# Gate rows replicated through the matrix engine, and bias bands written one group at a time, in a hybrid mLSTM and attention layer

## The chip, the cores and the metric

The kernel runs on one core of a Trainium2 chip. The metric is device time in microseconds of one execution of the whole layer. TensorE (PE, with its weight loads PEld), VectorE (DVE), ScalarE (ACT) and GpSimd (POOL) each work through an instruction queue of their own, in order; SyncE (SP) issues the weight loads from device memory, and POOL issues the other DMAs.

## The reference, cut to what matters

One layer over 256 tokens of width 1024, in float32. A combined projection feeds two mixers; the change touches the operands of both.

```
mLSTM (4 heads x 256):  d[q,s] = F[q] - F[s] + i[s]      (F: running sum of log f)
                        m[q]   = running maximum, the stabiliser
                        w[q,s] = exp(d[q,s] - m[q]) for s <= q
                        h      = (q k^T * w) v / max(|sum|, exp(-m))
attention (8 heads x 128): p = softmax(q k^T / sqrt(128) + bias[head, q - k]), causal
                           bias from a 32-bucket table of distances
x <- LayerNorm(a x + mixer(x));  x <- LayerNorm(a x + conv-gated MLP(x))
```

In the kernel G = i - F and M is the running maximum of G, so the weight of a pair is exp(G[s] - M[q]). It needs -M along the free axis, the same in all 128 partitions, a row of 256 numbers for each of the 4 heads. The bias of two attention heads is a tile `toe` of 128 x 2 x 256: partition p holds the bias row shifted by p places.

## The kernel before, in words

The weights come as 66 blocks of 1 MB, in the order of a list ("steps"): 4 blocks `o`, then four groups of eight (`qm`, `qb`, `km`, `kb`, `vm`, `vb`, `ga`, `gb`), then the branch and output projections and the MLP. A group is one mLSTM head and two attention heads. In step s PE multiplies block s with the activations; each matrix is split into a high and a low part (`wh`, `wl`), by ACT and DVE, two steps ahead, and a product is three matmuls (`mm3`, L124 to L126). SP loads block s+5 in step s into one of three `raw` buffers.

All orders are written by hand. For each step there is a list of element-wise work (`side_elem`, or a `mixed` list that interleaves it with the split), which is issued to ACT, DVE and POOL before the step's matmuls, and a list of small matmuls (`side_pe`) that PE does behind the step's own. Below, "b+4" is the fifth step of a group, its `vm`.

- `rel_bias_expand`, in step 4 (the first group's `qm`): DVE writes the table `ev`; POOL sends it to device memory (`table`, L499) and issues four copies there (`band`, L501), one for each group, in which each of the group's two rows is repeated 128 times. `load_band` (L354) reads a band with a row length one shorter than it was written with, which gives the shift by partition, into `toe`. For group 0 it stands in `open_att`, which runs when step 8 begins, for the others in b+1.
- `gates_schedule`: `e1d` (step b+2 of group 0) makes -M on DVE (L548, 4 x 256). POOL sends it to device memory (`rowscr`, L552) and reads it back into all partitions (`nM`, 128 x 4 x 256, L554).
- `group_schedule`, side work of PE: in b+4 `pe_s` (scores `pss`) and `pe_l(0)` (logits `psl` of the first attention head); in b+5 `pe_l(1)` and `pe_n` (the mLSTM's `psn`, from `sph`, `spl` and `vmh`, `vml`); in b+6 `pe_t` (`pst`).
- In b+5 the element-wise order is: `vtmp` (DVE); `el_w` (ACT's two Exp of `nM` give `wt`, L599 and L600, then POOL's causal mask, L601); `el_l(0)` (DVE adds `toe` to the logits, L702); the split of `vtmp`; `el_e(0)` (ACT); `el_s` (DVE multiplies `wt` with the scores, L608; ACT rounds to `sph`, L612); `el_l2(0)`; `el_s2` (`spl`); then `floor` and the split of a weight block.

Small results of PE go through five PSUM buffers in turn (`ps_side`), the steps' own through three others. `att`, the pool of `toe`, `wt`, `lg` and the like, opens in step 8, where the space of the pool `pre` becomes free.

Of the kernel before, what the change touches and what calls it, by code (L numbers as in the profile page):

```python
# [10 lines left out]
F32 = mybir.dt.float32  # L11
# [3 lines left out]
ALU = mybir.AluOpType  # L15
# [3 lines left out]
P = 128  # L19
S = 256  # L20
D = 1024
KT = D // P
NG = 4
# [8 lines left out]
LTOE = 384  # L32
# [37 lines left out]
class Kernel:  # L70
# [100 lines left out]
    def run(self):  # L171
        tc, nc, ctx = self.tc, self.nc, self.ctx
# [3 lines left out]
        dram = ctx.enter_context(tc.tile_pool(name="dram", bufs=1, space=DRAM))  # L176
# [6 lines left out]
        mp = mix_cm.__enter__()  # L183
# [53 lines left out]
        g = nc.gpsimd  # L237
# [18 lines left out]
        g.memset(self.vml[:, :, 256:258].bitcast(F32), 0.0)  # L256
        self.cbuf = mp.tile([P, 2, S + 3], F32, name="cbuf")
        g.memset(self.cbuf[:, :, 0:3], 0.0)
        self.cv = {n: mp.tile([P, 2, S], F32, name="cv" + n) for n in ("qm", "km")}
        self.ones4 = xp.tile([4, 2 * S], F32, name="ones4")  # L260
        g.memset(self.ones4[:, 0:S], 1.0)
# [19 lines left out]

        self.bands = [dram.tile([2, P * LTOE], F32, name=f"band{i}") for i in range(NG)]
        self.table = dram.tile([8, LTOE], F32, name="table")
        self.rowscr = dram.tile([4, S], F32, name="rowscr")

        att_cm = tc.tile_pool(name="att", bufs=1)
        post_cm = tc.tile_pool(name="post", bufs=1)
# [57 lines left out]
    def open_att(self, ap):  # L345
        self.ap = ap
        self.pt = [(ap.tile([P, 2, P], F32R, name=f"pth{i}"), ap.tile([P, 2, P], F32R, name=f"ptl{i}"),
                    ap.tile([P, P], F32, name=f"ptf{i}")) for i in range(2)]
        self.load_band(0)

    def load_band(self, g):
        self.toe = self.ap.tile([P, 2, S], F32, tag="toe", name=f"toe{g}", bufs=1)
        src = self.bands[g][:, 127:127 + P * (LTOE - 1)].rearrange("h (p c) -> p h c", c=LTOE - 1)
        self.nc.gpsimd.dma_start(self.toe, src[:, :, 0:S])  # L354

# [129 lines left out]
    def rel_bias_expand(self, rel, onehot):  # L485
        nc = self.nc
        st = {}

        def pe():
            ps = self.ps_side([8, LTOE], "ps_rel")  # L490
            nc.tensor.matmul(ps, rel, onehot, start=True, stop=True)
            st["ps"] = ps

        def elem():
            ev = self.xp.tile([8, LTOE], F32, name="ev")
            nc.vector.tensor_scalar(ev, st["ps"], 1.0 / ATT_SCALE, None, op0=ALU.mult)
            nc.vector.memset(ev[:, 256:LTOE], NEG)

            nc.gpsimd.dma_start(self.table, ev)  # L499
            for i in range(NG):  # L500
                nc.gpsimd.dma_start(self.bands[i].rearrange("h (p c) -> h p c", p=P),  # L501
                                    self.table[2 * i:2 * i + 2, :].unsqueeze(1).to_broadcast([2, P, LTOE]))
        self.side_pe.setdefault(3, []).append(pe)
        self.side_elem.setdefault(4, []).append(elem)


    def gates_schedule(self, bif):
        nc, mp = self.nc, self.xp
        st = {}
        v = nc.vector  # L510

        def e0():
            gt = mp.tile([P, 2, 8], F32, name="gt")
            for t in range(2):
                v.tensor_add(gt[:, t, :], self.psg[t][:, 256:264], bif)
            st["gt"] = gt

        def p0():
            ps = self.ps_side([4, 2, S], "ps_gt")
            for w in range(2):  # L520
                for t in range(2):
                    nc.tensor.transpose(ps[:, w, t * P:(t + 1) * P], st["gt"][:, t, 4 * w:4 * w + 4], self.ident)
            st["ps"] = ps

        def e1():
            ps = st["ps"]
            big = mp.tile([P, KT, S], F32, tag="xraw", name="gates")
            fs, t1, F, G, M, nFM, nM = (big[0:4, k, :] for k in range(7))
            v.tensor_copy(fs, ps[:, 1, :])
            v.scalar_tensor_tensor(t1, fs, -1.0, fs, op0=ALU.mult, op1=ALU.min)  # L530
            nc.scalar.activation(t1, t1, AF.Exp)
            nc.scalar.activation(t1, t1, AF.Ln, bias=1.0)
            st["g"] = fs, t1, F, G, M, nFM, nM

        def e1b():
            fs, t1, F, G, M, nFM, nM = st["g"]
            one = self.ones4[:, 0:S]
            v.scalar_tensor_tensor(fs, fs, 0.0, t1, op0=ALU.min, op1=ALU.subtract)
            v.tensor_tensor_scan(F, one, fs, 0.0, op0=ALU.mult, op1=ALU.add)

        def e1c():
            fs, t1, F, G, M, nFM, nM = st["g"]
            v.tensor_sub(G, st["ps"][:, 0, :], F)
            v.tensor_tensor_scan(M, self.ones4[:, S:2 * S], G, 0.0, op0=ALU.max, op1=ALU.max)

        def e1d():
            fs, t1, F, G, M, nFM, nM = st["g"]
            v.tensor_scalar(nM, M, -1.0, None, op0=ALU.mult)  # L548
            v.scalar_tensor_tensor(nFM, F, -1.0, M, op0=ALU.mult, op1=ALU.subtract)
            st.update(G=G, nFM=nFM)  # L550

            nc.gpsimd.dma_start(self.rowscr, nM)  # L552
            self.nM = self.mp.tile([P, 4, S], F32, name="nM")
            nc.gpsimd.dma_start(self.nM, self.rowscr.unsqueeze(0).to_broadcast([P, 4, S]))  # L554

        def p1():
            ps = self.ps_side([P, 2, 2, 4], "ps_gc")
            for w, n in enumerate(("G", "nFM")):
                for t in range(2):
                    nc.tensor.transpose(ps[:, w, t, :], st[n][:, t * P:(t + 1) * P], self.ident[0:4, 0:4])  # L560
            st["gc"] = ps

        def e2():
            self.gcol = self.const.tile([P, 2, 4], F32, name="gcol")
            self.floor = self.const.tile([P, 2, 4], F32, name="floor")
            v.tensor_copy(self.gcol, st["gc"][:, 0])
            self.floor_exp = lambda: nc.scalar.activation(self.floor, st["gc"][:, 1], AF.Exp)

        b = self.start_g[0]
        self.side_elem.setdefault(b, []).append(e0)  # L570
        self.side_pe.setdefault(b, []).append(p0)
        self.mixed[b + 1] = lambda w: w + [None, None, e1]
        self.mixed[b + 2] = lambda w: w + [e1b, None, e1c, None, e1d]
        self.side_pe.setdefault(b + 3, []).append(p1)
        self.mixed[b + 4] = lambda w: w + [e2]


    def group_schedule(self, g):
        nc = self.nc
        v, a = nc.vector, nc.scalar  # L580
        st = {}
        b = self.start_g[g]

        def pe_s():
            qh, ql = self.hl["qm"]
            kh, kl = self.hl["km"]
            pss = self.ps_side([P, 2, S], f"pss{g}")
            for k in range(2):
                self.mm3(pss[:, 1, :], kh[:, k, 0:P], kl[:, k, 0:P], qh[:, k, :], ql[:, k, :], k == 0, k == 1)

            for k in range(2):
                nc.tensor.matmul(pss[:, 0, P:], self.cv["km"][:, k, P:], self.cv["qm"][:, k, P:],
                                 start=k == 0, stop=k == 1)
            st["pss"] = pss

        def el_w():
            wt = self.ap.tile([P, 3, P], F32, tag="wt", name=f"wt{g}")
            psw = self.nM[:, g, :]
            a.activation(wt[:, 0, :], psw[:, P:], AF.Exp, bias=self.gcol[:, 1, g:g + 1])  # L599
            a.activation(wt[:, 1:3, :], psw, AF.Exp, bias=self.gcol[:, 0, g:g + 1])  # L600
            nc.gpsimd.affine_select(wt[:, 0:2, :], wt[:, 0:2, :], pattern=[[0, 2], [1, P]], base=0,  # L601
                                    channel_multiplier=-1, compare_op=ALU.is_ge, fill=0.0)
            st["wt"] = wt
# [80 lines left out]
        def pe_l(i):  # L684
            qh, ql, qf = self.qb
            kh, kl = self.hl["kb"]
            ps = self.ps_side([P, 2, S], f"psl{g}_{i}")
            self.mm3(ps[:, 1, :], qh[:, i, :], ql[:, i, :], kh[:, i, :], kl[:, i, :], True, True)

            nc.tensor.matmul(ps[:, 0, 0:P], qf[:, i, :], self.kbf[:, i, :], start=True, stop=True)  # L690
            st["l", i] = ps
# [61 lines left out]
        def at(where, k, f):  # L753
            where.setdefault(b + k, []).append(f)

        if g:
            at(self.side_elem, 1, lambda: self.load_band(g))
        at(self.side_pe, 4, pe_s)
        at(self.side_pe, 4, lambda: pe_l(0))
        at(self.side_pe, 5, lambda: pe_l(1))  # L760
        at(self.side_pe, 5, pe_n)
        self.mixed[b + 5] = lambda w: [w[0], el_w, lambda: el_l(0), w[1], lambda: el_e(0), el_s, lambda: el_l2(0),
                                       el_s2] + w[2:]
        if g == 0:
# [387 lines left out]
```

## Time and profile before

| | |
|---|---|
| time, median of 3 runs (lowest, highest) | 505.64 us (504.04, 506.53) |
| time of the profiled execution | 504.9 us |
| its span, first to last instruction | 503.0 us |
| PE busy | 487.5 us, 97% |
| DVE busy | 370.0 us, 74% |
| ACT busy | 289.0 us, 57% |
| POOL busy | 32.3 us, 6% |
| mean granted TensorE clock | 0.989 |

The busy times are of the profiled execution and refer to its span; the 1.9 us between span and time lie outside the instructions. In the views, a clock of 1.00 is 2.4 GHz and 0.50 is 1.2 GHz. "Waits" name the engine that stood idle, the line it then ran, and what released it. A duration behind a DMA's issue on POOL is the issue alone; its landing is told apart.

### The profile page before, as it was taken

The numbers are of one execution on the slowest core, as the hardware profiler recorded it, in microseconds if no ns is written. First come the engines' busy times: TensorE is split into PE (matmuls) and PEld (weight loads), VectorE is DVE, ScalarE is ACT, GpSimd is POOL, SyncE is SP. The second block draws the span as 40 slices with busy tenths as digits, with TensorE's granted clock in tenths as the row PEclk, the third lists the DMA queues.
The fourth block names the chain that finished last, engine by engine and source line by source line (L and its number), as shares of the span: only waits on it lengthen the run. The fifth ranks groups of instructions, "written<-read, shape, count | busy, mean of one in ns | idle before, by whom it ended". The sixth has DMA issues, their size and how long they took to land.

```text
span 503.0 us, 9460 instructions
## 1 busy us (share of the span) xinstructions
PE 487.5 (97%) x3881; PEld 471.3 (94%) x3881; DVE 370.0 (74%) x662; ACT 289.0 (57%) x478; POOL 32.3 (6%) x46
## 2 busy tenths in 40 slices
PE   8999969999999999999999999999999999999992
PEld 4999969999999999999999999999999999999982
DVE  5677946877687768786667788878668666866776
ACT  6657646577657665866645542766455545654620
POOL 0503101000100010001100001000000000000001
PEclk9999988999999999999999999999999999999998
DMA  8995745444544454544874481827464446454202
GB/s 254 343 319 161 248 149 188 168 169 168 189 168 169 167 190 168 173 168 163 298 287 169 168 328 46 297 85 251 168 234 171 182 168 223 170 194 168 85 0 83
DMA packets 19212, 94.27 MB, mean 187 GB/s; under 512 B 4669, under 2 KB 5961, under 8 KB 9185
## 3 DMA queue, kind: packets, MB, share of 16 engines
q1 hardware_dynamic: 14834, 87.08, 47.8%
q0 software_dynamic: 4336, 6.59, 4.4%
q8 instruction: 30, 0.49, 0.4%
q14 instruction: 12, 0.10, 0.1%
HBM read 92.58 MB, written 2.64 MB: 189 GB/s over the span
## 4 chain that ended last, share of the span: by engine, by line
PE 90%; DVE 4%; DMA 3%; ACT 1%; issue 0%; POOL 0%; SPq 0%; DVEq 0%; POOLq 0%
PE ps_up L126 8%; PE ps_up L124 8%; PE ps_up L125 8%; PE ffn L126 4%; PE ffn L125 4%; PE ffn L124 4%; DMA raw<-in_wst_dram 2%; PE ps_ga L126 2%; PE ps_ga L124 2%; PE ps_ga L125 2%; PE ps_qm L124 2%; PE ps_gb L126 1%; PE ps_gb L124 1%; PE ps_gb L125 1%; PE ps_qm L126 1%; PE ps_qm L125 1%
## 5 line engine op out<-in xcount | busy, mean ns | idle before, releaser
L92 DVE TENSOR_TENSOR wl<-raw,wh 128x1024 fp32r<-128x1024 f32 (+1 forms) x162 | 188.0, 1200 | 28.4 <-ACT wh L91 27.9
L91 ACT CAST wh<-raw 128x1024 fp32r<-128x1024 f32 (+1 forms) x162 | 158.9, 1031 | 11.5 <-DMA raw<-in_wst_dram 7.0
L124 PE MATMUL ps_up<-x1h,wh 128*128 128x256 f32 x320 | 90.0, 281 | 0.0
L125 PE MATMUL ps_up<-x1l,wh 128*128 128x256 f32 x320 | 89.9, 281 | 0.0
L126 PE MATMUL ps_up<-x1h,wl 128*128 128x256 f32 x320 | 89.9, 281 | 0.0
L125 PEld LDWEIGHTS ps_up<-x1l,wh 128*128 128x128 f32 x320 | 61.3, 192 | 0.0
L126 PEld LDWEIGHTS ps_up<-x1h,wl 128*128 128x128 f32 x320 | 60.2, 188 | 0.0
L124 PEld LDWEIGHTS ps_up<-x1h,wh 128*128 128x128 f32 x320 | 60.1, 188 | 0.0
L985 DVE SCALAR_TENSOR_TENSOR cu<-ps_up,vec,cu 128x255 f32<-128x255 f32 (+1 forms) x80 | 33.1, 476 | 27.0 <-ACT cu L981 26.9
L126 PE MATMUL ffn<-wh,hl 128*128 128x512 f32 (+1 forms) x110 | 38.4, 349 | 0.0
L125 PE MATMUL ffn<-wl,hh 128*128 128x512 f32 (+1 forms) x110 | 38.4, 349 | 0.0
L124 PE MATMUL ffn<-wh,hh 128*128 128x512 f32 (+1 forms) x110 | 38.3, 349 | 0.0
L91 ACT CAST hh<-cu 128x256 fp32r<-128x256 f32 x22 | 9.0, 408 | 42.9 <-DVE cu L993 42.9
L981 ACT ACTIVATE cu<-ps_up,vec 128x256 f32<-128x256 f32 x40 | 16.8, 472 | 28.7 <-PE ps_up L126 27.9
L125 PEld LDWEIGHTS ffn<-wl,hh 128*128 128x128 f32 x110 | 20.8, 189 | 3.0
L124 PEld LDWEIGHTS ffn<-wh,hh 128*128 128x128 f32 x110 | 20.7, 188 | 3.0
L126 PEld LDWEIGHTS ffn<-wh,hl 128*128 128x128 f32 x110 | 20.7, 188 | 2.9
L124 PE MATMUL ps_ga<-xth,wh 128*128 128x256 f32 x64 | 18.8, 294 | 0.0
L125 PE MATMUL ps_ga<-xtl,wh 128*128 128x256 f32 x64 | 18.8, 293 | 0.0
L126 PE MATMUL ps_ga<-xth,wl 128*128 128x256 f32 x64 | 18.8, 293 | 0.0
L892 POOL TENSOR_TENSOR rs<-rs,mhalf 128x1 f32<-128x1 f32 x4 | 2.7, 667 | 247.5 <-DVE rs L891 247.5
L124 PE MATMUL ps_vb<-wh,xth 128*128 128x256 f32 x64 | 18.3, 286 | 0.0
(288 smaller groups left out, 1450.9 us busy)
## 6 DMA issues: line engine op xcount, KB each, us to landing
raw<-in_wst_dram SPq DMA_DIRECT2D x78, 1024.0 KB, 4.9
raw<-in_wst_dram SPq DMA_DIRECT2D x8, 256.0 KB, 4.3
lnrow<-in_rows_dram POOLq DMA_DIRECT2D x4, 512.0 KB, 6.8
band<-table POOLq DMA_DIRECT2D x4, 384.0 KB, 14.2
xraw<-in_xt_dram SPq DMA_DIRECT2D x8, 128.0 KB, 4.2
raw<-in_wst_dram SPq DMA_DIRECT2D x2, 512.0 KB, 7.5
toe<-band POOLq DMA_DIRECT2D x4, 256.0 KB, 4.7
xtok<-in_x_dram POOLq DMA_DIRECT2D x1, 1024.0 KB, 8.0
```

Source lines behind the costliest of these rows:

```text
L91: self.nc.scalar.copy(wh, raw)
L92: self.nc.vector.tensor_sub(wl, raw, wh.bitcast(F32))
L124: mm(ps, ah, bh, start=start, stop=False)
L125: mm(ps, ah, bl, start=False, stop=False)
L126: mm(ps, al, bh, start=False, stop=stop)
L892: nc.gpsimd.tensor_tensor(st["rs"], st["rs"], self.mhalf[:, 0:1], op=ALU.pow)
L981: act.activation(cu[:, j, :], ps[:, j, :], AF.Copy, scale=tap(2, j))
L985: v.scalar_tensor_tensor(cu[:, j, o:], ps[:, j, :S - o], tap(t, j), cu[:, j, o:], op0=ALU.mult, op1=ALU.add)
```

## The change

-M of the four heads is written by DVE into the first four partitions of a 128 x 256 tile, whose other partitions POOL has set to zero at the start. For each group, at the head of the side work of b+4, one float32 matmul (`pe_m`) multiplies that tile with column g of the identity, read as a 128 x 128 matrix with the column repeated; each partition of the result `psw` (PSUM) is row g. `el_w` reads `psw` in place of `nM`. The way through device memory (`rowscr`) goes away.

`toe` becomes one tile of the long-lived pool. The copy into a band is issued for group 0 right behind the table, followed at once by `load_band(0)`; the copy for group g+1 stands in b+6 of group g.

```diff
+        self.nM = mp.tile([P, S], F32, name="nM")
+        g.memset(self.nM, 0.0)
+        self.toe = mp.tile([P, 2, S], F32, name="toe")
...
-        self.rowscr = dram.tile([4, S], F32, name="rowscr")
...
-        self.load_band(0)
+
+    def copy_band(self, g):
+
+        self.nc.gpsimd.dma_start(self.bands[g].rearrange("h (p c) -> h p c", p=P),
+                                 self.table[2 * g:2 * g + 2, :].unsqueeze(1).to_broadcast([2, P, LTOE]))
 
     def load_band(self, g):
-        self.toe = self.ap.tile([P, 2, S], F32, tag="toe", name=f"toe{g}", bufs=1)
...
-            for i in range(NG):
-                nc.gpsimd.dma_start(self.bands[i].rearrange("h (p c) -> h p c", p=P),
-                                    self.table[2 * i:2 * i + 2, :].unsqueeze(1).to_broadcast([2, P, LTOE]))
+            self.copy_band(0)
+            self.load_band(0)
...
-            v.tensor_scalar(nM, M, -1.0, None, op0=ALU.mult)
+            v.tensor_scalar(self.nM[0:4, :], M, -1.0, None, op0=ALU.mult)
...
-            nc.gpsimd.dma_start(self.rowscr, nM)
-            self.nM = self.mp.tile([P, 4, S], F32, name="nM")
-            nc.gpsimd.dma_start(self.nM, self.rowscr.unsqueeze(0).to_broadcast([P, 4, S]))
...
+        def pe_m():
+
+            psw = self.ps_side([P, S], f"psw{g}")
+            nc.tensor.matmul(psw, self.ident[:, g:g + 1].to_broadcast([P, P]), self.nM, start=True, stop=True)
+            st["psw"] = psw
...
-            psw = self.nM[:, g, :]
+            psw = st["psw"]
...
+        if g < NG - 1:
+            at(self.side_elem, 6, lambda: self.copy_band(g + 1))
+        at(self.side_pe, 4, pe_m)
```

On POOL, from the table to the first group's mask and its `scl` (a small power, L660 before and L666 after), stood before:

```order
L499 DMA table<-ev 8x384
L501 DMA band_203<-table 256x1x384
L501 DMA band_204<-table 256x1x384
L501 DMA band_205<-table 256x1x384
L501 DMA band_206<-table 256x1x384
L552 DMA rowscr<-gates 4x256
L554 DMA nM<-rowscr 128x1024
L354 DMA toe_724<-band_203 128x2x256
L601 AFFINE_SELECT wt_795<-wt_795 128x256
L660 ISA
L660 TENSOR_TENSOR scl_901<-scl_901,mhalf 128x2
```

and stands now:

```order
L504 DMA table<-ev 8x384
L355 DMA band_206<-table 256x1x384
L360 DMA toe<-band_206 128x2x256
L607 AFFINE_SELECT wt_792<-wt_792 128x256
L355 DMA band_207<-table 256x1x384
L666 ISA
L666 TENSOR_TENSOR scl_898<-scl_898,mhalf 128x2
```

Three band copies, `rowscr` and `nM` no longer stand ahead of the first load of `toe`; the second band's copy stands behind the first mask.

On PE, behind the last matmuls of the first group's `vm` in b+4, stood before:

```order
L126 MATMUL ps_vm_728<-wh_549,xtl 128x256
L124 MATMUL pss_778<-qmh,kmh 128x256
L125 MATMUL pss_778<-qml,kmh 128x256
L126 MATMUL pss_778<-qmh,kml 128x256
L124 MATMUL pss_778<-qmh,kmh 128x256
```

and stands now:

```order
L126 MATMUL ps_vm_723<-wh_549,xtl 128x256
L587 MATMUL psw_773<-nM,ident 128x256
L124 MATMUL pss_775<-qmh,kmh 128x256
L125 MATMUL pss_775<-qml,kmh 128x256
L126 MATMUL pss_775<-qmh,kml 128x256
L124 MATMUL pss_775<-qmh,kmh 128x256
```

One row is new, ahead of the scores; the same row is new in each of the other three groups, four in all.

## Rows read from the trace of the kernel before

**Rows 1.** The page: busy us by engine, share of the span, instructions.

```profile
PE 487.5 (97%) x3881; PEld 471.3 (94%) x3881; DVE 370.0 (74%) x662; ACT 289.0 (57%) x478; POOL 32.3 (6%) x46
```

**Rows 2.** Longest wait of PE: line, what released it, us in total, times, longest.

```profile
PE psn L124 <- ACT sph L612: 4.4, 1, 4.4
```

**Rows 3.** Stretches: length; busy us of PE, PEld, DVE, ACT, POOL; clock, DMA share, GB/s.

```profile
40.00:42.00 2.00, 2.00 (x20) 2.00 (x19) 2.00 (x4) 1.51 (x2) 2.00 (x3) 1.00 0.07 10
...
70.00:72.00 2.00, 0.00 (x0) 0.00 (x0) 1.91 (x8) 0.99 (x5) 0.00 (x0) 0.98 0.00 0
72.00:78.00 6.00, 5.44 (x24) 5.28 (x25) 5.54 (x21) 3.71 (x9) 0.00 (x0) 0.50 0.14 41
...
100.00:250.00 150.00, 150.00 (x1301) 150.00 (x1300) 114.01 (x235) 102.81 (x187) 9.37 (x11) 1.00 0.51 179
```

**Rows 4.** Timeline of PE, group 0: start, us, line, operation, idle before.

```profile
67.80 0.39 PE L690 MATMUL psl<-kbf,qbf 128*128 128x128 f32 x2
72.56 0.58 PE L124 MATMUL psn<-vmh,sph 128*128 128x258 f32 x1 [4.37 <-ACT sph L612]
...
82.29 0.82 PE L722 MATMUL pst<-ident,lg 128*128 128x128 f32 x6
```

**Rows 5.** Timeline of PE, the same places of group 1.

```profile
125.21 0.39 PE L690 MATMUL psl<-kbf,qbf 128*128 128x128 f32 x2
...
132.17 0.82 PE L722 MATMUL pst<-ident,lg 128*128 128x128 f32 x6
```

**Rows 6.** Timeline of ACT, group 0.

```profile
59.63 1.07 ACT L91 CAST wh<-raw 128x1024 fp32r<-128x1024 f32 x1
66.87 1.28 ACT L599 ACT_TABLE_LOAD   x1 [6.17 <-DMA nM<-rowscr]
...
68.47 0.49 ACT L600 ACTIVATE wt<-nM,gcol 128x256 f32<-128x256 f32 x1
...
72.00 0.51 ACT L612 CAST sph<-wt 128x384 fp32r<-128x384 f32 x1
```

**Rows 7.** Timeline of DVE, group 0.

```profile
62.39 0.67 DVE L450 TENSOR_TENSOR vtmp<-ps_vm,bvm 128x512 f32<-128x512 f32 x1
70.06 0.29 DVE L702 CUSTOM_DVE_ANT_0 lg<-psl,toe 128x128 f32<-128x128 f32 x1 [6.99 <-DMA toe<-band]
```

**Rows 8.** Timeline of POOL, from the bands to the end of group 0.

```profile
39.75 4.33 POOL L501 DMA_DIRECT2D band<-table  x4 [3.83 <-DMA table<-ev]
...
61.93 0.60 POOL L554 DMA_DIRECT2D nM<-rowscr  x1 [8.33 <-DMA rowscr<-gates]
62.80 0.74 POOL L354 DMA_DIRECT2D toe<-band  x1 [0.27 <-DMA raw<-in_wst_dram]
...
80.35 1.58 POOL L660 TENSOR_TENSOR scl<-scl,mhalf 128x2 f32<-128x2 f32 x1 [10.89 <-DVE scl L659]
```

**Rows 9.** Landing of the four band copies, by tile.

```profile
DMA to landing us min/median/max: 13.4/14.2/18.4
```

**Rows 10.** DMA issues from 35 to 64 us: KB each, median us to landing.

```profile
raw<-in_wst_dram SPq DMA_DIRECT2D x4, 1024.0 KB, 7.6
...
toe<-band POOLq DMA_DIRECT2D x1, 256.0 KB, 7.0
```

**Rows 11.** Timeline of ACT, group 1: the rounding and the next weight cast.

```profile
121.34 0.51 ACT L612 CAST sph<-wt 128x384 fp32r<-128x384 f32 x1
121.76 2.00 ACT L91 CAST wh<-raw 128x1024 fp32r<-128x1024 f32 x2
```

**Rows 12.** Timeline of SP's queue from 105 to 122 us.

```profile
105.64 12.14 SPq L86 DMA_DIRECT2D raw<-in_wst_dram  x3
```

**Rows 13.** The chain that ended last: one float32 product of 128 columns.

```profile
119.14 0.22 PE psl L690 x2
```

**Rows 14.** The same view: one float32 product of 384 columns.

```profile
30.87 0.74 PE ps_rel L491 x2
```

**Rows 15.** Weight loads of the float32 logits product: us in all, mean ns.

```profile
L690 PEld LDWEIGHTS psl<-kbf,qbf 128*128 128x128 f32 x16 | 2.5, 190 | 0.0
```

## The prediction

> **What bounds the kernel now.** I read the page first: PE is busy for 97% of the span [rows 1], so the time is PE's own work plus the places where PE stands still or runs slowly. The waits of PE come next, and there is one of size: 4.4 us ahead of `psn`, released by ACT's `sph` [rows 2]. Then the stretches. From 100 to 250 us PE has no gap in 150 us, at a clock of 1.00; around the wait it does nothing from 70 to 72 us, and when it resumes the clock is 0.50 (1.2 GHz) from 72 to 78 us, after 0.98 in the stretch ahead [rows 3]. The wait is thus paid twice, once as idle time and once as slow matmuls behind it.
>
> To price both at once I compare the same stretch of two groups, which hold the same PE work: from the last logits product (L690) to the first transpose (L722). Group 0 takes 82.29 - 67.80 = 14.49 us [rows 4], group 1 takes 132.17 - 125.21 = 6.96 us [rows 5]. The difference is **7.53 us**: 4.37 of idle time and 3.16 of the low clock.
>
> What was late? PE waited for `sph`, which ACT made at 72.00 to 72.51 [rows 6]. Followed back, there are two late inputs. ACT stood 6.17 us until `nM` had landed and loaded its Exp table at 66.87 [rows 6]; DVE stood 6.99 us until `toe` had landed and began the logits at 70.06 [rows 7]. The later one is `toe`, and it set the end: all of ACT's Exp work on `wt` was over at 68.96 (68.47 + 0.49) [rows 6]. Both are late because of POOL's queue. `nM` is issued at 61.93, after 8.33 us of waiting for `rowscr`; `toe` stands behind it and is issued at 62.80 [rows 8], though its band had been asked for at 39.75 and the first copies took some 13.4 us [rows 8, 9]. So faster rows of -M alone would not shift the end; moving `toe` ahead is half of the matter.
>
> **The change, part by part.** *The stall goes.* For -M, ACT is free at 60.70 (59.63 + 1.07); the Exp table and the two Exp took 66.87 to 68.96, 2.09 us [rows 6], so `wt` is ready at about 62.8. The new product needs DVE's -M, which POOL had sent off before 53.6 (61.93 - 8.33) [rows 8]. PE does it ahead of the scores and of the whole next step, 48 products; 57 of these make the 6.96 us of group 1, so a step is some 5.9 us, and `psw` is ready before 67.80 - 5.9 = 61.9, while ACT still loads its table (until 61.98). For `toe`, the first band copy is issued at 39.75 as now [rows 8]. How long a lone copy takes no row shows. The slowest of four sharing copies took 18.4 us, the fastest 13.4 [rows 9], and the load of `toe` 7.0 us beside `nM` and a weight block [rows 10]. At the worst of these it lands at 39.75 + 18.4 + 7.0 = 65.2, with the fastest copy at 60.2; alone on the queue it should be earlier still. DVE is free for the logits at 63.06 (62.39 + 0.67) [rows 7]. From the logits to the end of `sph` it took 72.51 - 70.06 = 2.45 us [rows 6, 7], so `sph` is ready at 65.5. PE begins L690 at 67.80 [rows 4], plus 0.44 for the new product, 68.24: a margin of 2.7 us. Group 1, where nothing is late, has 125.21 - 121.85 = 3.4 us [rows 5, 11], which fits. So `toe` may land as late as 65.8 before PE feels it, and the worst sum of rows is 65.2. I take the whole 7.53 us as gone, with no new stall in its place.
>
> *Four products on PE are added*, one per group, and PE has no gap to hide them in [rows 3], so a price of nothing is excluded. A float32 product with 128 moving columns is two passes and holds PE for 0.22 us [rows 13]; with 256 columns I take 0.44. The product with 384 columns took 0.74 [rows 14], which scales to 0.49 and unscaled is an upper end. A weight matrix that repeats one column no row shows; a float32 weight load lasts 190 ns [rows 15] and is hidden behind the product ahead; should both of a product stay uncovered, 0.38 comes on top. So each costs 0.44, between 0.43 and 0.74 + 0.38 = 1.12; four cost **1.76 us**, between 1.7 and 4.5. I stay at the low end, since the 128-column row is the same operation on full partitions.
>
> *Moved at no cost.* POOL's zeroing of the new tile lies at the start, where POOL later waits for the table anyway. ACT reads `psw` from PSUM instead of `nM` from SBUF; the 2.7 us of margin cover any difference. The three later band copies are issued behind the mask of each group, in the 10.89 us for which POOL waits for `scl` [rows 8]; each issue takes 1.08 us (4.33 / 4). Without that cover `scl` would be 1.08 us late in each group. Each of these copies has until the next group's logits, some 50 us after it, against 18.4 + 7.0. While it runs, a weight block may land later: 7.6 us in the stretch with the old copies [rows 10]. A block asked for at 105.64 [rows 12] is read by ACT three casts later, at 121.76 [rows 11]: 16.1 us, so the weights stay hidden. Behind the waiting load of `toe` only POOL's next mask is queued, which in group 0 is wanted at about 63.
>
> *The sum*: -7.53 + 1.76 = **-5.77 us**. From the profiled execution's own 504.9 us that gives 499.1. This execution lies 0.7 under the median of 505.64, inside the runs shown; the mean of the four is 505.3, and from there I get **499.5 us**. PE is the bound from there to the end, so what group 0 gives back is not lost later.
>
> **A rule against it.** While the bands are issued DVE is busy for 2.00 of 2 us and the DMA engines move 10 GB/s [rows 3], so the copies start slowly; whether the other copies or DVE are to blame, the rows don't tell. The Trainium skill, page "SBUF — State Buffer", section "SBUF: two separate sides", says that GpSimd cannot write the descriptors of a DMA that it issues while DVE holds the port pair they share, so that such a transfer seems to stall. By that rule the lone band would be no faster than 13.4 us and `toe` would land at 60.2 rather than near 50; both are ahead of 65.8, so the sum is the same, but it is why I give the slower rival below 4 in 100 and not 2.
>
> **The rivals.** (a) *The stall shrinks but stays*: `toe` lands between 65.8 and 70. For it speaks that POOL waits in order for the table, the band and `toe`; against it, the 65.2 of the worst rows. Each us costs one, and as the clock was still 0.98 in the stretch before PE resumed [rows 3], a short stall costs only itself. `toe` at 68 gives 2.2 us: 501.7. (b) *The products are dear*: at 1.12 us each, 505.3 - 7.53 + 4.5 = 502.2. The gain drops under 0.5% (2.5 us) when one costs more than (7.53 - 2.5) / 4 = 1.26 us. (c) *The same stall*: the change doesn't bring `toe` forward, and it lands at 70.06 as now; the first product hides in the stall, three don't: 505.3 + 1.3 = 506.6. (d) *Slower*: the band's copy, starved while POOL issues it, holds up `toe` until after 71.3 us; there the time passes 507.8, 0.5% over. The chain from 39.75 would have to last 31.5 us against 25.4 at the worst of rows 9 and 10.
>
> **How the numbers follow.** About 2.5 us, 0.5%, is what a measurement of this kernel can tell from no change. The forecast, 498 to 500.5, gets 0.73; (a) 0.10, (b) 0.07, (c) 0.06, (d) 0.04. Faster by over 0.5% (under 503.1) are the forecast, (b) and about half of (a): 0.85; within 0.5% the rest of (a) and (c): 0.11; slower 0.04. The low end is the fastest run with the cheapest products, 504.04 - 7.53 + 1.7 = 498.2, less 0.4 for a stretch that gives a little more: 497.8. The high end takes in (b) and the larger part of (a): 502.8.
>
> **What would show it.** Right: no wait of PE at `psn`; a clock of 1.00 from 60 to 90 us; L690 to L722 of group 0 in about 7.0 us; `toe` landed before 63; four `psw` products of about 0.44 us; a span of about 497.3. Wrong: a wait of DVE for `toe` in group 0 that reaches beyond 65.8, PE waiting ahead of `psw` or `pss`, a product of over 1 us, or casts that wait for `raw` behind a band copy.

## The result, and the profile after

The changed kernel takes 500.66 us (median of 5 runs, 498.91 to 501.06) against 505.64 us; the ratio is 0.9901, with a 95% interval of 0.9873 to 0.9929. That is 5.0 us less, between 3.6 and 6.4. The profiled execution took 500.76 us with a span of 498.7 us. Executions of one kernel can lie in two groups some 4 us apart (last section), so differences of one or two us are read below from the traces, stretch by stretch, and not from medians.

All waits of PE in the changed kernel (they answer to [rows 2]):

```profile
PE ps_o L156 <- ACT wh L91: 1.8, 2, 1.2
PE warm_ps L193 <- DVE warm L190: 1.2, 1, 1.2
PE ps_o L125 <- DVE wl L92: 0.7, 2, 0.4
```

The wait at `psn` is gone; what is left lies in the first steps. The timeline of PE in group 0, at the places of [rows 4]:

```profile
69.76 0.39 PE L696 MATMUL psl<-kbf,qbf 128*128 128x128 f32 x2
...
76.72 0.82 PE L728 MATMUL pst<-ident,lg 128*128 128x128 f32 x6
```

From the last logits product to the first transpose it is 76.72 - 69.76 = 6.96 us, to the hundredth what group 1 took before [rows 5], in place of 14.49 [rows 4]. The stretches (length; busy us of PE, PEld, DVE, ACT, POOL; clock, DMA share, GB/s) answer to [rows 3]:

```profile
70.00:72.00 2.00, 2.00 (x19) 2.00 (x18) 1.97 (x11) 0.81 (x4) 0.00 (x0) 1.00 0.13 55
72.00:78.00 6.00, 6.00 (x54) 6.00 (x53) 5.25 (x18) 3.07 (x7) 0.73 (x1) 1.00 0.52 204
```

PE has no gap and the clock stays at 1.00. ACT and DVE, timelines of group 0, as [rows 6, 7]:

```profile
62.26 1.28 ACT L605 ACT_TABLE_LOAD   x1
...
66.48 0.51 ACT L618 CAST sph<-wt 128x384 fp32r<-128x384 f32 x1
```

```profile
63.92 0.67 DVE L456 TENSOR_TENSOR vtmp<-ps_vm,bvm 128x512 f32<-128x512 f32 x1
64.53 0.27 DVE L708 CUSTOM_DVE_ANT_0 lg<-psl,toe 128x128 f32<-128x128 f32 x1
```

Neither waits for a transfer any more. `sph` is ready at 66.99, 2.77 us before PE's last logits product at 69.76. And POOL, as [rows 8]:

```profile
41.34 1.15 POOL L355 DMA_DIRECT2D band<-table  x1 [3.89 <-DMA table<-ev]
55.19 0.76 POOL L360 DMA_DIRECT2D toe<-band  x1 [12.71 <-DMA band<-table]
64.41 0.42 POOL L607 TENSOR_SCALAR_AFFINE_SELECT wt<-wt 128x256 f32<-128x256 f32 x1 [8.46 <-DMA raw<-in_wst_dram]
64.95 1.12 POOL L355 DMA_DIRECT2D band<-table  x1
75.71 0.73 POOL L666 TENSOR_TENSOR scl<-scl,mhalf 128x2 f32<-128x2 f32 x1 [9.64 <-issue]
80.03 0.90 POOL L360 DMA_DIRECT2D toe<-band  x1 [3.59 <-DMA band<-table]
```

The DMA issues of the first band and of `toe` (KB each, us from issue to landing):

```profile
band<-table POOLq DMA_DIRECT2D x1, 384.0 KB, 13.6
...
toe<-band POOLq DMA_DIRECT2D x1, 256.0 KB, 4.3
```

`toe` is issued at 55.19 in place of 62.80 and lands 4.3 us later, at 59.5; DVE wants it at 64.53. Two things are to be seen: POOL stood 12.71 us until a *lone* band copy had landed, so the copy is hardly quicker alone (13.6 us against 13.4 to 18.4 [rows 9]); and the second group's load waits for its own copy, at a place where that costs nothing. (The mask at 64.41 follows ACT's second Exp, which ends at 64.29; the transfer of `raw` named there is only what the profile saw last.)

The new product, from the chain that ended last (start, us):

```profile
61.76 0.43 PE psw L587 x2
```

**The account of the profiled executions.** The stretch gives back 7.53 us. The four products take 4 x 0.43 = 1.73. The changed kernel's L696 stands 1.96 us later than L690 did (69.76 against 67.80 [rows 4]), of which 0.43 are the first product; the other 1.53 us were lost before the change begins to act: POOL's `table` already leaves at 36.92 in place of 35.39. How early group 0 comes varies from execution to execution: the same kernel, profiled again, has its L696 at 67.85. Together -7.53 + 1.73 + 1.53 = -4.27, and the spans differ by 503.0 - 498.7 = 4.3 us.

### The profile page after: what moved, and what is told of

It is laid out like the page before. It is cut to its first block, busy times and chain, and to the rows that moved or that the text cites. A ratio compares the mean times of both kernels' runs of the same rounds, so it can differ in the third digit from the quotient of the medians.

```text
span 498.7 us, 9469 instructions
## 1 busy us (share of the span) xinstructions
PE 485.6 (97%) x3889; PEld 469.1 (94%) x3889; DVE 370.2 (74%) x662; ACT 288.3 (58%) x478; POOL 29.7 (6%) x45
## 4 chain that ended last, share of the span: by engine, by line
PE 94%; DMA 2%; DVE 1%; SPq 1%; issue 1%; ACT 0%; POOL 0%; POOLq 0%
PE ps_up L126 8%; PE ps_up L125 8%; PE ps_up L124 8%; PE ffn L126 4%; PE ffn L125 4%; PE ffn L124 4%; DMA raw<-in_wst_dram 2%; PE ps_vm L124 2%; PE ps_vb L125 2%; PE ps_ga L125 2%; PE ps_vb L124 2%; PE ps_ga L126 2%; PE ps_qm L124 2%; PE ps_ga L124 2%; PE ps_vb L126 2%; PE ps_vm L125 2%
## 5 line engine op out<-in xcount | busy, mean ns | idle before, releaser
L126 PEld LDWEIGHTS ps_up<-x1h,wl 128*128 128x128 f32 x320 | 60.2, 188 | 0.0
L124 PE MATMUL ps_gb<-xth,wh 128*128 128x256 f32 x64 | 18.0, 282 | 0.0
L124 PE MATMUL ps_vm<-wh,xth 128*128 128x256 f32 x64 | 18.0, 282 | 0.0
L125 PE MATMUL ps_vb<-wl,xth 128*128 128x256 f32 x64 | 18.0, 281 | 0.0
```

The source lines that it names most:

```text
L124: mm(ps, ah, bh, start=start, stop=False)
L125: mm(ps, ah, bl, start=False, stop=False)
L126: mm(ps, al, bh, start=False, stop=stop)
```

## The experiments

Ratios are to the kernel before, run beside each kernel on the same chip; the first four runs share one chip, the last four another, so their times are not set side by side. "Stretch" is the time from group 0's last logits product to its first transpose: 14.49 before, 6.96 after.

**One half alone: the copies are spread.** The gates' rows still go through device memory, and `toe` is loaded where it was.

```diff
...
-            for i in range(NG):
-                nc.gpsimd.dma_start(self.bands[i].rearrange("h (p c) -> h p c", p=P), ...)
+            self.copy_band(0)
...
+        if g < NG - 1:
+            at(self.side_elem, 6, lambda: self.copy_band(g + 1))
```

> The kernel before with one half of the change alone: the band copies of groups 1 to 3 go to b+6 of the group ahead; the gates' rows still travel through device memory and toe is still loaded when step 8 begins. Theory (the two late inputs were late because rowscr, nM and toe stood in one POOL queue behind four band copies that kept the DMA engines): rowscr lands some 4 us after its issue at about 53 instead of 8.7, nM by about 62, toe by about 64; PE waits under 0.5 us at psn, the stretch of group 0 from the last logits product to the first transpose takes 7.0 to 7.5 us, and with no new product on PE the time is 6.5 to 7.5 us under the kernel before, ratio 0.985 to 0.987. Rival 1 (both halves are needed, as the prediction said): toe still lands after 66, the stall stays at 2 us or more, ratio 0.992 or more. Rival 2 (the gain is not the stall at all): ratio 1.00.

Measured: 495.59 us, ratio 0.9864 (0.9815 to 0.9913). POOL's and PE's timelines:

```profile
59.29 0.58 POOL L556 DMA_DIRECT2D nM<-rowscr  x1 [4.59 <-DMA rowscr<-gates]
60.24 0.74 POOL L358 DMA_DIRECT2D toe<-band  x1 [0.38 <-ACT kbf L440]
```

```profile
68.91 0.39 PE L692 MATMUL psl<-kbf,qbf 128*128 128x128 f32 x2
69.83 0.39 PE L124 MATMUL psn<-vmh,sph 128*128 128x258 f32 x1 [0.54 <-ACT sph L614]
...
76.85 0.81 PE L724 MATMUL pst<-ident,lg 128*128 128x128 f32 x6
```

With three copies out of the way POOL waits 4.59 us for `rowscr` in place of 8.33 [rows 8], and `toe` leaves at 60.24. The stretch is 7.94 us, a little over the 7.0 to 7.5 expected: 0.54 of waiting is left, and about as much in the next products. What comes last there is no longer `toe` but the rows: ACT waits 3.62 us for `nM` and loads its Exp table only at 65.43, and DVE's split of `vtmp` then waits 1.10 us for ACT. This half takes away 6.6 of the 7.5 us, without a product on PE.

**The other half alone: the rows go through PE.** All four copies stand at once behind the table, and `toe` is loaded when step 8 begins, as before.

```diff
-            self.copy_band(0)
-            self.load_band(0)
+            for i in range(NG):
+                self.copy_band(i)
...
     def open_att(self, ap):
...
+        self.load_band(0)
```

> The changed kernel with the other half alone: the gates' rows go through PE, but all four band copies are issued at once behind the table, and toe is loaded when step 8 begins, into the tile it had before. Theory (POOL's queue made toe late): toe is issued when its band has landed, near 55 instead of 62.8, and lands by 62; no wait at psn, time as that of the whole change, ratio 0.988 to 0.992. Rival (toe is late because four copies share the engines, both halves needed): DVE waits for toe until 66 or later, stretch of group 0 over 8 us, ratio 0.993 or more.

Measured: 496.13 us, ratio 0.9868 (0.9818 to 0.9919). POOL and PE:

```profile
42.05 4.33 POOL L355 DMA_DIRECT2D band<-table  x4 [5.22 <-DMA table<-ev]
56.63 0.76 POOL L361 DMA_DIRECT2D toe<-band  x1 [10.24 <-DVE cvkm L408]
```

```profile
69.15 0.39 PE L697 MATMUL psl<-kbf,qbf 128*128 128x128 f32 x2
...
76.11 0.82 PE L729 MATMUL pst<-ident,lg 128*128 128x128 f32 x6
```

The stretch is 6.96 us and PE does not wait. Without `rowscr` and `nM` in POOL's queue `toe` leaves at 56.63, though four copies run as before; it lands 6.9 us later, near 63.5 and not by 62, which is still in time. The ratio lies under the 0.988 to 0.992 expected; the last section shows why the ratio says little here. Either half alone takes away most of the stall or all of it; the rival that both are needed fell in both runs.

**Another form of the copy.** The kernel before, with the 128 repeats as the outer dimension.

```diff
-                nc.gpsimd.dma_start(self.bands[i].rearrange("h (p c) -> h p c", p=P),
-                                    self.table[2 * i:2 * i + 2, :].unsqueeze(1).to_broadcast([2, P, LTOE]))
+                nc.gpsimd.dma_start(self.bands[i].rearrange("h (p c) -> p h c", p=P),
+                                    self.table[2 * i:2 * i + 2, :].unsqueeze(0).to_broadcast([P, 2, LTOE]))
```

> The kernel before with one other edit: each band copy is written with the 128 repeats as its outermost dimension and the two heads inside, instead of the other way; same bytes, same number of copies, nothing else moved, no product added on PE. In the changed kernel a lone copy still took 13.6 us at a DMA share of 0.1 to 0.2, some two of sixteen engines. If the order of the dimensions spreads a copy over the engines, each lands in 3 to 6 us, rowscr lands in about 4 us, toe by 64, there is no wait at psn, and the time is 6.5 to 7.5 us under the kernel before (ratio 0.985 to 0.987). If DVE holds up the descriptors instead, the copies still take 12 us or more and the stall of 4.4 us stays (ratio 0.999 to 1.001).

Measured: 496.89 us, ratio 0.9868 (0.9817 to 0.9919). The landing of its four copies (by tile), and a stretch in which they run:

```profile
DMA to landing us min/median/max: 4.6/6.2/8.3
```

```profile
42.00:44.00 2.00, 2.00 (x20) 2.00 (x19) 2.00 (x2) 0.27 (x1) 2.00 (x4) 1.00 0.36 115
```

Four at once land in 4.6 to 8.3 us (3 to 6 expected) in place of 13.4 to 18.4 [rows 9], with DVE busy for 2.00 of 2 us while they are issued. The queue of the DMAs that POOL issues (q0: packets, MB, share of 16 engines) shows the difference: first the lone copy of the old form in the changed kernel, from 41.5 to 55 us, then the four copies of the new form, from 41.5 to 48 us, the last not quite done.

```profile
q0 software_dynamic: 704, 0.40, 10.4%
```

```profile
q0 software_dynamic: 347, 1.28, 63.2%
```

A share of 10.4% of 16 engines is 1.7 engines on the mean, where the four new copies together take 10.1. A lone copy of the new form, in the last run below, landed in 4.5 us; from 41 to 42 us it had a DMA share of 1.00, at 253 GB/s, with DVE busy for 1.00 of 1 us:

```profile
band<-table POOLq DMA_DIRECT2D x1, 384.0 KB, 4.5
```

So the form is what made a copy slow, and not DVE: the old form was slow in the changed kernel also from 45 to 49 us, when DVE was busy for 0.75 of 4 us and the copy moved 0.19 MB, or 48 GB/s. The number of packets does not explain it either: 637 of the 704 had gone by 45 us, and the last 67, with 0.30 MB, took ten us. What is left of the causes named here is the number of engines, which the shares bear out but no view lists engine by engine.

The Trainium skill, page "DMA: Bandwidth & Descriptors", section "Why a DMA increments its semaphore by 16 and not by 1", says that a transfer goes to the largest number of engines up to 16 that divides the outermost dimension (of a size other than 1) of both sides. By that the old form, with 2 outermost, gets two engines and the new one, with 128, all 16; the mean share of 1.7 engines and the share of 1.00 agree, though a share of packet time is not a count of engines: it was 29% from 43 to 45 us, with the many small packets. (The expectation above read the whole DMA share of 0.1 to 0.2 as the copy's; from 51 to 53 us 8.9% of the 0.13 were a weight block and 4.5% the copy.)

The stretch is 76.28 - 68.54 = 7.74 us, so this edit of two lines takes away 6.75 of the 7.53 us, with 0.17 us of waiting left at `psn`; `toe` landed at about 66 rather than by 64:

```profile
68.54 0.39 PE L690 MATMUL psl<-kbf,qbf 128*128 128x128 f32 x2
...
76.28 0.82 PE L722 MATMUL pst<-ident,lg 128*128 128x128 f32 x6
```

**The changed kernel beside them.** No edit.

> The changed kernel once more, on the chip and beside the runs of the other three: ratio 0.990, within 0.987 to 0.993. If four products cost 1.7 us and nothing else separates it from the two kernels without them, it stands 1.7 us above whichever of those has no stall.

Measured: 499.0 us, ratio 0.9890 (0.9835 to 0.9945). Its stretch is 74.81 - 67.85 = 6.96 us:

```profile
67.85 0.39 PE L696 MATMUL psl<-kbf,qbf 128*128 128x128 f32 x2
...
74.81 0.82 PE L728 MATMUL pst<-ident,lg 128*128 128x128 f32 x6
```

The ratio is as forecast, but the intervals of the four overlap, and the 1.7 us of the products cannot be read from them: the run with the rows alone has the same four products and the same stretch of 6.96 us, and stands at 0.9868.

**Each product four times.**

```diff
+            for _ in range(4):
                 nc.tensor.matmul(psw, self.ident[:, g:g + 1].to_broadcast([P, P]), self.nM, ...)
```

> The changed kernel with each of the four new products done four times over into the same PSUM tile, 16 in place of 4. Theory (a product holds PE for its two passes, 0.43 us, with nothing hidden and no weight load uncovered): 12 more cost 5.2 us; the stretch from the last vm matmul to the first score matmul is 4 x 0.43 = 1.73 us. Rival (dear products, 0.74 to 1.12 us each): 8.9 to 13.4 us more. Rival (hidden): under 1 us more.

Measured: 505.73 us, ratio 1.0038 (0.9998 to 1.0079), which is 1.4% or 6.9 us over the changed kernel's 0.9901. With both intervals together that is some 4.4 to 9.4 us (an estimate, as for two independent runs): the 5.2 us forecast lie inside, the 1 us of hidden products does not, but the 8.9 us of the cheapest dear product lie just inside too. The time alone therefore does not settle it; the chain shows the price:

```profile
60.62 1.73 PE psw L588 x8
```

Eight passes take 1.73 us, 0.43 for one product, so the dear products are out. No weight load adds time to that, though the matrix repeats one column.

**`toe` late on purpose.** In the changed kernel DVE sets `toe` to zero seven times behind `vtmp`, and the load waits for that.

```diff
-            self.load_band(0)
...
+        def el_late():
+            for _ in range(7):
+                v.memset(self.toe, 0.0)
+            self.load_band(0)
...
```

> The changed kernel with the first load of toe made late on purpose: DVE sets toe to zero seven times, behind the vtmp of group 0, and the load can only start then. toe should land some 8 us later than DVE wants it. Theory (the margin at psn is 2.7 us, and a stall of more than 4 us is paid twice): PE idles 4 to 6 us at psn, the clock then falls to 0.50 and the stretch from the last logits product to the first transpose is 6.96 + the idle time + about 3 us, 14 to 16 us in all. Rival (the low clock of the kernel before had another cause than the idle time): the clock stays 1.00 and the stretch is 11 to 13 us.

Measured, one execution: 507.09 us. PE waits, and the clock falls while it does:

```profile
PE psn L124 <- ACT sph L617: 5.0, 1, 5.0
```

```profile
70.00:72.00 2.00, 0.00 (x0) 0.00 (x0) 0.37 (x3) 0.00 (x0) 0.59 (x1) 0.98 0.38 114
72.00:74.00 2.00, 0.00 (x0) 0.00 (x0) 1.93 (x8) 1.42 (x6) 0.00 (x0) 0.50 0.22 50
...
76.00:78.00 2.00, 2.00 (x12) 2.00 (x11) 2.00 (x6) 0.03 (x1) 0.00 (x0) 0.50 0.13 51
```

```profile
68.72 0.39 PE L695 MATMUL psl<-kbf,qbf 128*128 128x128 f32 x2
...
83.00 0.82 PE L727 MATMUL pst<-ident,lg 128*128 128x128 f32 x6
```

The stretch is 83.00 - 68.72 = 14.28 us, 7.32 over 6.96: 5.03 of idle time and 2.29 behind it, under the 3 expected. That is the picture of the kernel before, made again with the rows in time: DVE waits 3.59 us for `toe` and begins the logits at 71.63. (POOL's mask, queued behind the load, was late as well, but done by 69.53.)

**The same, once.** DVE sets `toe` to zero one time.

> The same with DVE setting toe to zero once, so that the load starts right behind vtmp and lands some 4 to 5 us after DVE wants it. Theory (margin of 2.7 us; a short stall costs only itself): PE idles 1.5 to 2.5 us at psn, the clock stays 1.00, the stretch is 8.5 to 9.5 us. Rival (any stall at this place brings the low clock): 0.50 behind it and 11 us or more. Rival (margin larger than worked out): no wait, 6.96 us.

Measured, one execution: 503.78 us.

```profile
PE psn L124 <- ACT sph L617: 2.5, 1, 2.5
```

```profile
70.00:72.00 2.00, 0.71 (x3) 0.51 (x4) 1.70 (x6) 1.93 (x6) 0.00 (x0) 1.00 0.13 46
72.00:74.00 2.00, 2.00 (x11) 2.00 (x11) 1.89 (x2) 1.03 (x2) 0.00 (x0) 0.55 0.12 51
74.00:76.00 2.00, 2.00 (x12) 2.00 (x12) 1.97 (x11) 0.73 (x3) 0.00 (x0) 0.60 0.29 62
```

```profile
68.28 0.39 PE L695 MATMUL psl<-kbf,qbf 128*128 128x128 f32 x2
...
79.77 0.82 PE L727 MATMUL pst<-ident,lg 128*128 128x128 f32 x6
```

PE idled 2.46 us, as worked out, but the clock then fell, after PE had resumed at 71.12: its means of 0.55 and 0.60 are mostly the lower level, 1.2 GHz. The stretch is 79.77 - 68.28 = 11.49 us, 4.53 over 6.96. The theory was right on the margin and wrong on the clock: this short stall too was paid twice. In the run with spread copies 0.54 us of waiting left the clock at 1.00 throughout.

**The rows through device memory, with `toe` early.** The changed kernel with the wide copy, and without the product; `rowscr` is read back one head at a time.

```diff
...
+    def load_row(self, g):
+        self.nc.gpsimd.dma_start(self.nM[:, g % 2], self.rowscr[g:g + 1, :].to_broadcast([P, S]))
...
+            nc.gpsimd.dma_start(self.rowscr, nM)
+            self.load_row(0)
+            self.load_row(1)
...
-        at(self.side_pe, 4, pe_m)
+        if g < 2:
+            at(self.side_elem, 6, lambda: self.load_row(g + 2))
```

> A version from the experiments: toe and its copies stand where the changed kernel has them, with the wide form of the copy; the gates' rows go through device memory again, but one head at a time into two buffers (heads 0 and 1 at once, 2 and 3 in b+6 of groups 0 and 1), and PE has no product. Theory (either way of bringing the rows in time is enough, and the products cost 1.7 us): toe lands before 55, the first row by 63, no wait at psn or under 0.3 us, stretch 6.96 to 7.3 us, time 7.5 us under the kernel before, ratio 0.984 to 0.987, and 1.7 us under the changed kernel. Rival (rows through device memory are too late for the first group whatever stands ahead of them): a stall of 0.5 to 1 us stays as in the runs with spread and with wide copies.

Measured: 494.14 us (493.12 to 498.49), ratio 0.9856 (0.9802 to 0.9910).

```profile
43.99 0.74 POOL L363 DMA_DIRECT2D toe<-band  x1 [4.00 <-DMA band<-table]
...
57.19 1.12 POOL L359 DMA_DIRECT2D nM<-rowscr  x2 [4.35 <-DMA rowscr<-gates]
```

```profile
67.05 0.39 PE L696 MATMUL psl<-kbf,qbf 128*128 128x128 f32 x2
67.34 0.39 PE L124 MATMUL psn<-vmh,sph 128*128 128x258 f32 x1
...
74.53 0.82 PE L728 MATMUL pst<-ident,lg 128*128 128x128 f32 x6
```

`toe` leaves at 43.99. The stretch is 7.48 us, over the 7.3 expected, though no wait of PE at `psn` is listed: ACT gets the first row only at about 62.9 (57.19 and 5.6 us to landing), so some 0.5 us is left, as the rival had it. By its trace it does 1.73 us less on PE than the changed kernel for 0.52 more in the stretch. It is ahead of the old kernel beyond its interval; against the other kernels here, the changed one (0.9890) among them, the intervals overlap, so that it is the better one is argued from the traces and not shown by the times.

## Why the prediction was right, point by point

- **The stall goes, and 7.53 us with it: right.** The stretch fell to 6.96 us and the clock stayed at 1.00. The margin was put at 2.7 us and is 2.77.
- **Four products cost 1.76 us: right**, 1.73 in the trace. The upper end, with weight loads uncovered, did not come.
- **"Faster rows of -M alone would not shift the end; moving `toe` ahead is half of the matter": wrong.** The prediction had itself read that `toe` stood behind `nM` and `rowscr` in POOL's queue. It did not draw the conclusion that taking these two out moves `toe` ahead by itself: 56.63 in the run with the rows alone. One queue was late, not two inputs for two reasons, and each edit that frees it takes away most of the stall: spreading the copies (stretch 7.94), widening them (7.74), or taking the rows out (6.96). What is left with spread copies hangs on the rows, which through device memory came a little late even with `toe` early (7.48).
- **"Alone on the queue it should be earlier still": wrong, at no cost.** A lone copy took 13.6 us, and later ones 12.1 to 14.5. `toe` landed at 59.5, close to the 60.2 worked out with 13.4, but partly by luck: the copy left 1.6 us later than assumed, and the load took 4.3 us instead of 7.0. The rule that was weighed against the change gave the right figure for the wrong reason: the wide copy, issued while DVE was as busy, shows that the form of the copy made it and not DVE. Rival (d), which rested on a starved copy, found no support in these runs.
- **The moved copies cost nothing: right.** POOL still waited 9.64 us ahead of the first `scl`, and from 35 to 110 us no cast waited for `raw`. The load of the second `toe`, put behind its copy, waited 3.59 us until 80.03 and landed 5.1 us later, 29 us before DVE began group 1's logits at 114.25.
- **The sum, -5.77 us: right within the noise.** The time gave -5.0 (-6.4 to -3.6), and the profiled spans -4.3, in which 1.53 us were lost in the first steps, ahead of anything that was changed. In the second set of runs it is -6.0 in either group of executions (last section).
- **Rival (a)'s price, "a short stall costs only itself": wrong.** A stall of 2.46 us cost 4.53. The price rested on a clock that was still 0.98 before PE resumed; the runs show that it can fall after that. Had `toe` been late by that much, the time would have been some 2 us over the price given there.

## What to carry to other kernels

When two inputs of a stage are late, look whether they wait in one queue: then one cause may stand behind both, and the cheapest edit that frees the queue can be nearly enough. Ask a slow DMA for its own queue's share of the engines before anything is built around it: at a tenth of 16, two exchanged dimensions brought nine tenths of what the whole change brought in the stretch, without a product on PE. On a kernel that PE bounds, idle time of PE can cost more than its length: the three stalls of 2.46 to 5.03 us here cost 1.5 to 1.8 times theirs, since the clock fell behind them.

## What the runs showed of the hardware

**The clock falls behind shorter stalls than expected.** Idle times of 5.03, 4.37 and 2.46 us were followed by stretches at or near 0.50 (1.2 GHz) and cost 7.32, 7.53 and 4.53 us in all; 0.54 us left the clock at 1.00. With 2.46 us the fall came only after PE had resumed. One execution of each stands behind this.

**The MLP runs at one of two paces.** In two executions the matmuls of the up projection had this cost (group of instructions from 300 to 480 us: busy us, mean ns), first in the changed kernel (the kernel before has the same line), then in the one with spread copies:

```profile
L124 PE MATMUL ps_up<-x1h,wh 128*128 128x256 f32 x320 | 90.0, 281 | 0.0
```

```profile
L124 PE MATMUL ps_up<-x1h,wh 128*128 128x256 f32 x320 | 88.4, 276 | 0.0
```

From group 1's first transpose to the last product it is 361.6 us in the kernel before and in the one with wide copies, but 357.1 in the one with spread copies, at a granted clock of 1.00. The runs of one kernel part in the same way: spread copies 494.95 to 496.15 and 498.86 to 499.25, the kernel before on the same chip 500.66 to 502.27 and 504.22 to 507.06. The profiled executions tie the groups to the pace: 281 ns at 498.85 us (changed kernel) and 498.95 (wide copies), 276 ns at 495.03 (spread copies) and 495.31 (rows alone).

Parted at that gap, which was done with the times in view, the first four runs agree with their traces. The means of the lower and of the upper group stand under the kernel before by 6.0 and 6.3 us with spread copies (6.55 by the stretch), 5.9 and 6.0 with the rows alone (5.80 by the stretch and the products), 6.5 and 6.7 with wide copies (6.75), and 6.0 and 6.0 for the changed kernel (5.80). So the ratios of 0.9868 and 0.9890 for two kernels with the same work on PE differ by how many of their six executions fell into either group. What sets the pace stayed open.
